# First norm from whole rows, roots by a square root and one Newton step, last product and store by tile, another order of recurrence pieces

## The chip, the cores and the metric

The kernel runs on one core of a Trainium2 chip. The metric is the device time of one execution in microseconds (us), taken as the median of several runs. Lower is better.

## The reference

A model of four blocks works on x of 512 tokens by 1024 values, all in float32. Each block is a mixer and then a feed-forward network, both behind a root-mean-square norm and both added to the running state h:

```python
for i in range(DEPTH):
    hn = rmsnorm(h, norm_mix[i])
    m = [rwkv7_mix, swa_sink_mix, sgu_chunk_mix, gla_mix][i](hn, ...)
    h = h + m
    h = h + swiglu(rmsnorm(h, norm_ffn[i]), ffn_w_in[i], ffn_w_out[i])
return rmsnorm(h, norm_final)

def rmsnorm(x, g):
    y = x * lax.rsqrt(jnp.mean(jnp.square(x), -1, keepdims=True) + 1e-5)
    return y * g
```

The first mixer holds a recurrence over the 512 tokens with 16 heads of 64; it is the part whose order of work is changed. The norm in front of it, and the norm behind the last feed-forward network, are the other two places of the change.

## The kernel before, in words

**Recorded and planned.** The program is first recorded: every operation becomes an object with its engine, its operands and an estimated cost. Then `Program.run` (lines 301 to 421) plans: it gives out the operations one by one, each time the one that can start earliest by its estimates, and on a tie the one recorded first. What it gives out is the order in which each engine then runs its own instructions, one after the other. So a line that is recorded earlier or later moves instructions on all engines. All recorded operations have line 239 in the profile. The planner also puts unneeded products of the identity matrix (line 525, called fillers below) on TensorE where it expects a gap, so that the engine's clock stays up.

**Split products.** Each float32 operand is split into a high part (a cast on ScalarE, tile `whi` or `slot`) and a low part (a subtraction on VectorE, tile `wlo` or `slot`), and `mm3` (line 613) makes three products of them. The feed-forward networks and three projections multiply 2 by 2 blocks with seven products in place of eight (`seven`, line 865). `x22` is the last of the seven; it is added into the PSUM tiles `p` of the two products before it, one for each of two token tiles b.

**First norm.** `token_squares` (line 755) loads x (token by feature) in eight pieces of 128 by 512. ScalarE squares and sums six of them, VectorE takes the statistics of the two of the last token tile. The mean squares `ms` of four token tiles go through `rsqrt` (line 733): a starting value from the bits and three Newton steps, ten small VectorE operations one behind the other. `rstd` (line 778) spreads the result `rcol` over the partitions with four transposes on TensorE; x transposed (`x_t`, tiles `h`) is multiplied by it, and the first real products follow. Between them `load_cols` (line 562) brings the gain vectors: two DMAs, two TensorE transposes, two VectorE copies to `vec`.

**Recurrence.** Four groups n of four heads go through generators: `ahead(n)` prepares the decays and keys (tiles `ew`, `et`, `qk`, `kb`), `solve(n)` makes products (tiles `pa`, `pr`), inverts triangular blocks (first eight ScalarE copies of 32 partitions, `et<-pa` or `et<-pr`, then a chain of small VectorE operations), `rwkv_chain` steps the state through four chunks (tiles `wu`, `vu`, `tok`, `st`), and `rwkv_out` norms its result (tiles `out`). The string `ORDERS[n]` (line 31) tells in which order these generators are advanced while group n's chain runs: c is a step of the chain, o a half of the output, p a piece of `solve(n + 1)`, q a piece of `ahead(n + 2)`, f one of `ahead(n + 1)`.

**Last norm and store.** `finish` (line 670) squares and sums each finished half row of h on ScalarE. `store` (line 1990) takes the token tiles in two halves: `rcol` of two tiles, then for each tile the left half times `rcol` and gain on VectorE, the right half times `rcol` on ScalarE, and a DMA of 128 by 1024 to `out`.

Of the kernel before, what the change touches and what calls it, by code (L numbers as in the profile page):

```python
# [17 lines left out]
P = 128  # L18
S = 512
D = 1024  # L20
# [3 lines left out]
NB = S // P  # L24
EPS = 1e-5
SLOTS = 45
PARTS = ((4, 5), (0, 1), (2, 3))
WIDTHS = (512, 512, 512, 512, 384, 384)
TABLES = {AF.Exp: "exp", AF.Ln: "ln", AF.Sigmoid: "sigmoid", AF.Tanh: "tanh", AF.Silu: "silu", AF.Gelu: "gelu", AF.Sin: "sin"}
# [477 lines left out]
class K:  # L507
# [84 lines left out]
        return self.ps.tile([P, S], F32, name="ps")  # L592


    def weights(self, view, nk, n, pool=False):
# [9 lines left out]
        (nc.gpsimd if pool else nc.vector).tensor_sub(lo[:, :m], raw[:, :m], hi[:, :m])  # L605
        r = lambda t: t[:, :m].rearrange("p (k n) -> p k n", k=nk)
        return r(hi), r(lo)

# [136 lines left out]
    def rcol(self, b0=0, b1=NB):  # L745

        nc = self.nc
        ms, col = [self.sm.tile([P, NB], F32, name=n)[:, :b1 - b0] for n in ("ms", "rcol")]
        ss = self.ss.rearrange("p (b n) -> p b n", b=NB)[:, b0:b1, :]
        nc.vector.tensor_add(ms, ss[:, :, 0], ss[:, :, 1])  # L750
        nc.vector.tensor_scalar(ms, ms, 1.0 / D, EPS, op0=ALU.mult, op1=ALU.add)
        self.rsqrt(col, ms)
        return col

    def token_squares(self):


        nc = self.nc
        ss, ms = self.sm.tile([P, 2 * NB], F32, name="ss2"), self.sm.tile([P, NB], F32, name="ms")
        st, mv = self.lay.tile([P, 2, 6], F32, name="xst"), self.lay.tile([P, 2], F32, name="xmv")  # L760
        for j in range(2):
            for b in range(NB):
                x = self.slot()
                nc.sync.dma_start(x, self.d['x'][b * P:(b + 1) * P, j * S:(j + 1) * S])
                if b == NB - 1:
                    nc.vector.bn_stats(st[:, j, :], x)
                else:
                    nc.scalar.activation(x, x, AF.Square, accum_out=ss[:, 2 * b + j:2 * b + j + 1])
        nc.vector.bn_aggr(mv, st)
        s2 = ss.rearrange("p (b n) -> p b n", b=NB)  # L770
        l = NB - 1
        nc.vector.scalar_tensor_tensor(ms[:, l:], mv[:, 0:1], mv[:, 0:1], mv[:, 1:2], op0=ALU.mult, op1=ALU.add)
        nc.vector.tensor_scalar(ms[:, l:], ms[:, l:], EPS, None, op0=ALU.add)
        nc.vector.tensor_add(ms[:, :l], s2[:, :l, 0], s2[:, :l, 1])
        nc.vector.tensor_scalar(ms[:, :l], ms[:, :l], 1.0 / D, EPS, op0=ALU.mult, op1=ALU.add)
        return ms

    def rstd(self, ms=None):


        nc = self.nc
        if ms is None:
            col = self.rcol()
        else:
            col = self.sm.tile([P, NB], F32, name="rcol")
            self.rsqrt(col, ms)
# [58 lines left out]
    def out_fast(self, w, nsub, x, last):  # L845

        nc = self.nc
        where = {'m1': [(0, 0, 1)], 'm2': [(0, 0, 1)], 'm5': [(1, 1, -1), (0, 1, -1)], 'm3': [(0, 1, -1)], 'm6': [(0, 1, -1)],
                 'm7': [(1, 1, -1)], 'm4': [(1, 0, 1)]}
        for name, ps in self.seven(w, S, x, nsub):  # L850
# [14 lines left out]
    def seven(self, w, W, x, nsub=4):  # L865

# [7 lines left out]
        nc = self.nc  # L874
        us = [(k, min(2, nsub - k)) for k in range(0, nsub, 2)]
# [11 lines left out]
                nc.gpsimd.dma_start(t, w[q][:, k * W:(k + n) * W], accum_op=ALU.add)  # L887

        def mm(key, ps, raw, first, last):
            xs = x(key)  # L890
# [22 lines left out]
        b = load(2)  # L913
        add(b, 0)
        r = banks()
# [101 lines left out]
    def rwkv(self, g, g_next, slots):  # L1017
# [16 lines left out]
        xq, tp = self.pool("xq", 8, tall), self.pool("tp", 3, tall)  # L1034

        hn = self.h
        ms = self.token_squares()
# [952 lines left out]
    def store(self):  # L1990

        nc = self.nc
        for half in range(2):
            col = self.rcol(half * 2, half * 2 + 2)
            for j in range(2):
                b = half * 2 + j
                l, r = self.h[b][:, :S], self.h[b][:, S:]
                nc.vector.scalar_tensor_tensor(l, l, col[:, j:j + 1], self.g[0], op0=ALU.mult, op1=ALU.mult)
                nc.scalar.activation(r, r, AF.Identity, scale=col[:, j:j + 1])
                nc.sync.dma_start(self.d['out'][b * P:(b + 1) * P, :], self.h[b])  # L2000


# [143 lines left out]
```

## Time and profile before

| what | value |
|---|---|
| time, median of 3 runs | 2394.17 us (2392.96 to 2395.63) |
| span of the profiled execution | 2393.6 us |
| instructions | 36634 |
| TensorE (PE) busy | 2352.7 us, 98% |
| VectorE (DVE) busy | 1934.0 us, 81% |
| ScalarE (ACT) busy | 1437.0 us, 60% |
| GpSimd (POOL) busy | 326.3 us, 14% |
| bytes moved by DMA | 404.23 MB, 169 GB/s on average |

The profiled execution has no separate timing: its own time is known by its span, 2393.6 us, which is 0.57 us below the median of the runs and lies among them.

How to read the rows that follow in the prediction. In the order of time (the timeline) a row is: start in us from the span's start, duration in us, engine, line, operation, what it writes, what it reads, how many; in brackets at the end the idle time of the engine before it and what ended that. A float32 product of the identity shows as two records. In the table by stages a row is: from and to, length, then for each engine its busy time and count, then the granted clock of TensorE (1.00 is full), the busy share of the DMA engines and GB/s. In the chain of waits a row is: start, duration, and the engine and tile on which the end of the program hung then. In the groups a row is: operation and shapes, count, busy us, mean ns of one.

### The profile page before, as it was taken

What the parts mean: (1) busy time and instruction counts of PE and PEld (TensorE: products, weight loads), DVE (VectorE), ACT (ScalarE), POOL (GpSimd) and SP (SyncE); (2) the same over time, 40 slices, a digit from 0 to 9 for tenths busy, and PEclk for the clock granted to TensorE, in tenths of its full rate; (3) what the DMA queues carried; (4) which work ended last, traced back from release to release, by engine and by line L of the source; (5) the groups of instructions that cost most, each with busy time, mean ns of one, the idle gap of its engine ahead of it and who ended that gap; (6) DMA issues with size and microseconds to landing.
All of it is one profiled execution on the core that took longest, in us unless ns stands there. A gap on an engine that the chain in (4) does not pass through costs nothing.

```text
span 2393.6 us, 36634 instructions
## 1 busy us (share of the span) xinstructions
PE 2352.7 (98%) x13524; PEld 1925.6 (80%) x13524; DVE 1934.0 (81%) x3261; ACT 1437.0 (60%) x2514; POOL 326.3 (14%) x398
## 2 busy tenths in 40 slices
PE   9999889999999999999999999999999999999998
PEld 8577777988888769888887888888888778988886
DVE  8577987887889878878699888886869978886868
ACT  4476765755556587555575444755557737755555
POOL 0000000221211001211111101121121101121110
PEclk9999999999999999999999999999999999999999
DMA  5220012998998326999988664899898758899985
GB/s 174 71 77 13 8 66 65 214 217 221 220 213 202 88 65 156 211 234 217 215 217 212 187 157 100 197 210 227 219 216 210 166 134 171 203 204 233 218 207 118
DMA packets 127603, 404.23 MB, mean 169 GB/s; under 512 B 14400, under 2 KB 17984, under 8 KB 127424
## 3 DMA queue, kind: packets, MB, share of 16 engines
q0 software_dynamic: 51840, 176.18, 41.2%
q1 hardware_dynamic: 75584, 225.72, 28.1%
q8 instruction: 106, 1.74, 0.3%
q14 instruction: 73, 0.60, 0.1%
HBM read 397.39 MB, written 2.10 MB: 167 GB/s over the span
## 4 chain that ended last, share of the span: by engine, by line
PE 83%; DVE 6%; ACT 5%; DMA 4%; issue 2%; SPq 0%; POOL 0%; DVEq 0%; ACTq 0%; POOLq 0%
PE ps L239 83%; DVE slot L239 2%; ACT slot L239 2%; DMA wraw<-ffn_w_a 2%; DMA wraw<-ffn_w_b 1%; DVE wlo L239 1%; ACT et L239 1%; ACT whi L239 1%; DVE h L239 1%; ACT vu L239 0%; ACT wu L239 0%; DMA wraw<-sg_w_o 0%; ACT L239 0%; DVE left L239 0%; DMA slot<-x 0%
## 5 line engine op out<-in xcount | busy, mean ns | idle before, releaser
L239 PE MATMUL ps<-whi,slot 128*128 128x512 f32 (+1 forms) x5072 | 1554.2, 384 | 3.6 <-DVE slot L239 3.1
L239 PEld LDWEIGHTS ps<-whi,slot 128*128 128x128 f32 x5072 | 943.3, 188 | 179.2 <-ACT whi L239 8.0
L239 ACT CAST whi<-wraw 128x1024 fp32r<-128x1024 f32 (+3 forms) x843 | 688.3, 836 | 565.4 <-PE ps L239 432.9
L239 DVE TENSOR_TENSOR wlo<-wraw,whi 128x1024 fp32r<-128x1024 f32 (+3 forms) x843 | 790.5, 954 | 256.6 <-ACT whi L239 254.8
L239 PE MATMUL ps<-wlo,slot 128*128 128x512 f32 (+1 forms) x2536 | 968.9, 382 | 1.8 <-DVE wlo L239 1.8
L239 PEld LDWEIGHTS ps<-wlo,slot 128*128 128x128 f32 x2536 | 476.5, 188 | 86.5 <-DVE wlo L239 6.6
L239 PE MATMUL ps<-slot,whi 128*128 128x512 f32 x688 | 217.1, 395 | 1.0 <-ACT slot L239 1.0
L239 DVE TENSOR_TENSOR slot<-ps,slot 128x512 f32<-128x512 f32 (+2 forms) x271 | 161.0, 608 | 48.4 <-PE ps L239 33.9
L239 ACT CAST slot<-left 128x512 fp32r<-128x512 f32 (+1 forms) x294 | 164.6, 589 | 53.4 <-PE ps L239 29.5
L239 DVE TENSOR_TENSOR slot<-left,slot 128x512 fp32r<-128x512 f32 (+1 forms) x294 | 183.4, 644 | 10.8 <-ACT slot L239 6.9
L239 DVE TENSOR_TENSOR h<-h,ps 128x512 f32<-128x512 f32 x240 | 159.7, 683 | 27.7 <-PE ps L239 25.2
L239 POOL DMA_DIRECT2D wraw<-ffn_w_a x128 | 109.7, 860 | 497.8 <-DVE wlo L239 415.1
L239 PEld LDWEIGHTS ps<-slot,whi 128*128 128x128 f32 x688 | 127.7, 188 | 32.7 <-DVE slot L239 2.6
L239 PE MATMUL ps<-slot,wlo 128*128 128x512 f32 x344 | 133.9, 391 | 0.0
L239 POOL DMA_DIRECT2D wraw<-ffn_w_b x64 | 54.9, 864 | 419.9 <-DVE slot L239 119.9
L239 ACT COPY slot<-ps 128x512 f32<-128x512 f32 (+1 forms) x144 | 78.4, 562 | 39.0 <-PE ps L239 36.9
L239 POOL DMA_DIRECT2D wraw<-ffn_o_a x64 | 54.6, 853 | 285.6 <-DVE wlo L239 151.9
L239 ACT COPY left<-ps 128x512 f32<-128x512 f32 x108 | 54.8, 558 | 57.0 <-PE ps L239 57.0
L239 PE MATMUL ps<-ident,slot 128*128 128x128 f32 x561 | 85.8, 277 | 0.9 <-DVE slot L239 0.6
L239 PEld LDWEIGHTS ps<-ident,slot 128*128 128x128 f32 x561 | 63.3, 140 | 26.0 <-DVE slot L239 12.9
L239 PEld LDWEIGHTS ps<-slot,wlo 128*128 128x128 f32 x344 | 64.5, 188 | 14.2 <-DVE wlo L239 0.8
L239 DVE SCALAR_TENSOR_TENSOR slot<-slot,ncol 128x512 f32<-128x512 f32 (+1 forms) x96 | 65.1, 701 | 9.2 <-ACT slot L239 9.0
(302 smaller groups left out, 2070.2 us busy)
## 6 DMA issues: line engine op xcount, KB each, us to landing
wraw<-ffn_w_a SPq DMA_DIRECT2D x128, 512.0 KB, 6.6
wraw<-ffn_w_a POOLq DMA_DIRECT2D x128, 512.0 KB, 6.9
wraw<-ffn_o_a SPq DMA_DIRECT2D x64, 512.0 KB, 5.1
wraw<-ffn_o_a POOLq DMA_DIRECT2D x64, 512.0 KB, 7.3
wraw<-ffn_w_b SPq DMA_DIRECT2D x64, 384.0 KB, 3.9
wraw<-ffn_w_b POOLq DMA_DIRECT2D x64, 384.0 KB, 6.4
wraw<-gla_w_p SPq DMA_DIRECT2D x24, 512.0 KB, 4.9
wraw<-gla_w_p POOLq DMA_DIRECT2D x24, 512.0 KB, 6.3
```

The lines of the kernel that those rows point to most:

```text
L239: op = self.add(eng.name, lambda: getattr(eng.target, what)(*map(real, args), **{k: real(a) for k, a in kw.items()}), *self.price(eng.name ...
```

## The change

Three places are changed.

**First norm.** x is loaded in four whole rows of 128 by 1024 into tiles of the pool `rk`. ScalarE squares tiles 0 and 2 whole; VectorE takes the statistics of tile 1; of tile 3 VectorE takes the left half and ScalarE the right. A new function `root` replaces `rsqrt` at this norm and at the last: ScalarE's square root, then on VectorE a reciprocal and one Newton step (four small operations). A one-element square root is put in front, so that the square root's table is loaded first.

**Last product and store.** In the very last feed-forward product the matmuls of `x22` are recorded with all of token tile 0 ahead of token tile 1. `store` takes the tiles as (0, 1), (2) and (3), each group with its own `root`.

**Order.** `ORDERS` changes for groups 0, 1 and 2.

```diff
-ORDERS = "ffppcpqcpqqcopcopcoo", "ppcpqcpqqcopcopcoo", "ppcpcpcopcopcoo", "cccococ"
+ORDERS = "ffppcpqcpqqcocppocoo", "ppcpqcqpqcopcpcooo", "ppcpccpopcopcoo", "cccococ"
...
+    def root(self, ms):
...
+        n = ms.shape[-1]
+        col, t = [self.sm.tile([P, NB], F32, name=x)[:, :n] for x in ("rcol", "root")]
+        nc.scalar.activation(t, ms, AF.Sqrt)
+        nc.vector.reciprocal(col, t)
+        nc.vector.tensor_mul(t, col, col)
+        nc.vector.scalar_tensor_tensor(t, ms, -0.5, t, op0=ALU.mult, op1=ALU.mult)
+        nc.vector.scalar_tensor_tensor(col, t, 1.5, col, op0=ALU.add, op1=ALU.mult)
+        return col
+
+    def token_squares(self, rows):
...
+        for b in range(NB):
+            x = rows[b]
+            nc.sync.dma_start(x, self.d['x'][b * P:(b + 1) * P, :])
+            if b % 2 == 0:
+                nc.scalar.activation(x, x, AF.Square, accum_out=ss[:, b:b + 1])
+            elif b == 1:
+                for j in range(2):
+                    nc.vector.bn_stats(st[:, j, :], x[:, j * S:(j + 1) * S])
+                nc.vector.bn_aggr(mv[:, 0, :], st)
+            else:
+                late = self.lay.tile([P, 1, 6], F32, name="xlate")
+                nc.vector.bn_stats(late[:, 0, :], x[:, :S])
+                nc.scalar.activation(x[:, S:], x[:, S:], AF.Square, accum_out=ss[:, b:b + 1])
+                nc.vector.bn_aggr(mv[:, 1, :], late)
...
-                for b in range(2):
-                    for k in range(n):
-                        c = slice(k * W, (k + 1) * W)
-                        self.mm3(ps[b], *self.pick(xs, k0 + k, b), hi[:, c], lo[:, c], first and k0 + k == 0, last and k0 + k == nsub - 1)
+                sides = [(b, k0 + k, hi[:, k * W:(k + 1) * W], lo[:, k * W:(k + 1) * W]) for b in range(2) for k in range(n)]
+                if end and key == 'x22':
+                    held += sides
+                    sides = sorted(held, key=lambda x: x[0]) if u == len(us) - 1 else []
+                for b, k, h, l in sides:
+                    self.mm3(ps[b], *self.pick(xs, k, b), h, l, first and k == 0, last and k == nsub - 1)
...
+        rows = [keepers.tile([P, 2 * S], F32, name="rk") for _ in range(NB)]
+        nc.scalar.activation(self.sm.tile([P, NB], F32, name="root")[:, :1], self.onec, AF.Sqrt)
+        ms = self.token_squares(rows)
...
-        for half in range(2):
-            col = self.rcol(half * 2, half * 2 + 2)
-            for j in range(2):
-                b = half * 2 + j
+        for b0, b1 in ((0, 2), (2, 3), (3, 4)):
+            col = self.root(self.mean_squares(b0, b1))
+            for b in range(b0, b1):
```

What the planner makes of it at the places of which the prediction speaks follows; a row is the line, the operation, what it writes and reads, the shape, and how often in a row.

VectorE at the program's start, before: the two copies of the gain vectors (`vec`) stand in the middle of the mean squares (`ms`), and ten small operations from `rcol` to `rcol` follow.

```order
L239 BN_AGGR xmv<-xst 128x2
L239 TENSOR_SCALAR ms<-ms 128x3
L239 SCALAR_TENSOR_TENSOR ms<-xmv 128x1
L239 COPY vec<-ps 128x128
L239 TENSOR_SCALAR ms<-ms 128x1
L239 COPY vec<-ps 128x128
L239 TENSOR_SCALAR rcol<-ms 128x4
L239 TENSOR_TENSOR rs_t<-rcol 128x4
```

The same place now:

```order
L239 BN_AGGR xst_147<-xlate 128x2
L239 COPY vec<-ps 128x128
L239 SCALAR_TENSOR_TENSOR ms<-xst_147 128x1
L239 COPY vec<-ps 128x128
L239 TENSOR_SCALAR ms<-ms 128x1
L239 SCALAR_TENSOR_TENSOR ms<-ss_132,ms 128x1
L239 RECIPROCAL rcol<-root 128x4
L239 TENSOR_TENSOR root<-rcol 128x4
L239 SCALAR_TENSOR_TENSOR root<-ms,root 128x4
L239 SCALAR_TENSOR_TENSOR rcol<-root,rcol 128x4
```

The copies of `vec` still stand in front of the last three steps to `ms`; behind them four operations are left in place of ten, and the reciprocal waits for ScalarE's square root. On TensorE the 33 fillers at the program's start still stand ahead of the two transposes that these copies read.

ScalarE in the recurrence, as the chain of group 1 begins (`et<-pa` are the copies for the inversion, `et<-ew` and `ew<-ew` belong to the preparation, `wu` and `vu` to the chain), before:

```order
L239 COPY vu<-ps 64x256
L239 ACTIVATE et<-pa,mk 32x16x16
L239 COPY et<-pa 32x16x16
L239 COPY out<-ps 128x256
L239 ACTIVATE et<-pa,mk 32x16x16
L239 COPY et<-pa 32x16x16
L239 ACTIVATE wu<-st_1206,pend 128x128
L239 ACTIVATE et<-pa,mk 32x16x16
L239 ACTIVATE wu<-st_1206,pend 128x128
L239 COPY vu<-ps 64x256
L239 ACTIVATE et<-ew 128x512 x2
L239 ACTIVATE ew<-ew,ka_1211,vec 128x512
```

The same place now:

```order
L239 ACTIVATE et<-ew 128x512 x2
L239 ACTIVATE ew<-ew,ka_1199,vec 128x512
L239 ACTIVATE out<-ps,vec 128x256 x2
L239 COPY et<-pa 32x16x16 x2
L239 ACTIVATE wu<-st_1188,pend 128x128 x2
L239 CAST rk<-out 128x256 x2
L239 COPY vu<-ps 64x256
L239 ACTIVATE et<-pa,mk 32x16x16 x2
L239 COPY out<-ps 128x256
L239 COPY et<-pa 32x16x16 x2
L239 ACTIVATE et<-pa,mk 32x16x16 x2
```

The three operations of the preparation moved from behind the copies `et<-pa` to ahead of them. Some 45 us earlier, in the chain of group 0, TensorE had these rows before:

```order
L239 MATMUL ps<-vu,tok 64x64 x4
L239 MATMUL ps<-wu,iv 64x64 x8
L239 MATMUL ps<-st_1175,qk 64x128 x4
L239 MATMUL ps<-v_1360,pr 64x64 x3
L239 MATMUL ps<-vu,tok 64x64 x4
```

and has these now:

```order
L239 MATMUL ps<-vu,tok 64x64 x4
L239 MATMUL ps<-wu,iv 64x64 x5
L239 MATMUL ps<-st_1163,qk 64x128
L525 MATMUL ps<-ident 128x128 x3
L239 MATMUL ps<-st_1163,qk 64x128 x3
L239 MATMUL ps<-wu,iv 64x64 x3
L239 MATMUL ps<-vu,tok 64x64 x4
```

Three fillers moved in between the chain's products with the state. Over the recurrence the planner places 30 fillers where it placed 28.

At the program's end ScalarE had, behind the last four squares, only the four scalings of `h`. Now it has:

```order
L239 ACTIVATE slot,ss_22907<-h 128x512 x4
L239 ACT_TABLE_LOAD
L239 ACTIVATE root<-ms 128x2
L239 ACTIVATE root<-ms 128x1
L239 ACTIVATE h<-h,rcol 128x512 x3
L239 ACTIVATE root<-ms 128x1
L239 ACTIVATE h<-h,rcol 128x512
```

The table load and all three square roots stand behind the square of the last tile. On TensorE the sorted `x22` comes out of the planner nearly as it was: of its 24 matmuls one stands two places further ahead (the first of the third weight piece into the first token tile), and the first token tile is still complete six matmuls ahead of the second, as before.

More of the change, by code (lines that the diff above doesn't have):

```diff
@@ L28 @@
 WIDTHS = (512, 512, 512, 512, 384, 384)
-TABLES = {AF.Exp: "exp", AF.Ln: "ln", AF.Sigmoid: "sigmoid", AF.Tanh: "tanh", AF.Silu: "silu", AF.Gelu: "gelu", AF.Sin: "sin"}
+TABLES = {AF.Exp: "exp", AF.Ln: "ln", AF.Sigmoid: "sigmoid", AF.Tanh: "tanh", AF.Silu: "silu", AF.Gelu: "gelu", AF.Sin: "sin", AF.Sqrt: "sqrt"}
 ALSO = {"exp": ("tanh",), "sigmoid": ("tanh",), "silu": ("sin", "tanh"), "gelu": ("tanh",)}
-ORDERS = "ffppcpqcpqqcopcopcoo", "ppcpqcpqqcopcopcoo", "ppcpcpcopcopcoo", "cccococ"
+ORDERS = "ffppcpqcpqqcocppocoo", "ppcpqcqpqcopcpcooo", "ppcpccpopcopcoo", "cccococ"
 LOCAL = "qqqqqaqaqaqaoaoooaoaoaoo"
@@ L592, in bank, with weights @@
         return self.ps.tile([P, S], F32, name="ps")
-    def weights(self, view, nk, n, pool=False):
+    def weights(self, view, nk, n):
         nc = self.nc
@@ L604, in weights @@
         nc.scalar.copy(hi[:, :m], raw[:, :m])
-        (nc.gpsimd if pool else nc.vector).tensor_sub(lo[:, :m], raw[:, :m], hi[:, :m])
+        nc.vector.tensor_sub(lo[:, :m], raw[:, :m], hi[:, :m])
         r = lambda t: t[:, :m].rearrange("p (k n) -> p k n", k=nk)
@@ L743, in rsqrt, with mean_squares @@
             nc.vector.scalar_tensor_tensor(y, t, 1.5, y, op0=ALU.add, op1=ALU.mult)
-    def rcol(self, b0=0, b1=NB):
+    def mean_squares(self, b0, b1):
         nc = self.nc
-        ms, col = [self.sm.tile([P, NB], F32, name=n)[:, :b1 - b0] for n in ("ms", "rcol")]
+        ms = self.sm.tile([P, NB], F32, name="ms")[:, :b1 - b0]
         ss = self.ss.rearrange("p (b n) -> p b n", b=NB)[:, b0:b1, :]
@@ L751, in rcol @@
         nc.vector.tensor_scalar(ms, ms, 1.0 / D, EPS, op0=ALU.mult, op1=ALU.add)
+        return ms
+    def rcol(self):
+        ms, col = self.mean_squares(0, NB), self.sm.tile([P, NB], F32, name="rcol")
         self.rsqrt(col, ms)
         return col
-    def token_squares(self):
+    def root(self, ms):
         nc = self.nc
-        ss, ms = self.sm.tile([P, 2 * NB], F32, name="ss2"), self.sm.tile([P, NB], F32, name="ms")
-        st, mv = self.lay.tile([P, 2, 6], F32, name="xst"), self.lay.tile([P, 2], F32, name="xmv")
-        for j in range(2):
[L762 to L775, printed above, removed]
@@ new lines, in root @@
+        n = ms.shape[-1]
[7 more added lines that the diff above has]
+    def token_squares(self, rows):
+        nc = self.nc
+        ss, ms = self.sm.tile([P, NB + 1], F32, name="ss1"), self.sm.tile([P, NB], F32, name="ms")
+        st, mv = [self.lay.tile([P, 2, n], F32, name=f"xst{n}") for n in (6, 2)]
+        for b in range(NB):
[12 more added lines that the diff above has]
+                nc.vector.bn_aggr(mv[:, 1, :], late)
+        nc.vector.scalar_tensor_tensor(ms[:, 1:2], mv[:, 0, 0:1], mv[:, 0, 0:1], mv[:, 0, 1:2], op0=ALU.mult, op1=ALU.add)
+        nc.vector.tensor_scalar(ms[:, 1:2], ms[:, 1:2], EPS, None, op0=ALU.add)
+        nc.vector.tensor_scalar(ms[:, 0:3:2], ss[:, 0:3:2], 1.0 / D, EPS, op0=ALU.mult, op1=ALU.add)
+        m = ms[:, 3:4]
+        nc.vector.scalar_tensor_tensor(m, mv[:, 1, 0:1], mv[:, 1, 0:1], mv[:, 1, 1:2], op0=ALU.mult, op1=ALU.add)
+        nc.vector.tensor_scalar(m, m, 0.5, EPS, op0=ALU.mult, op1=ALU.add)
+        nc.vector.scalar_tensor_tensor(m, ss[:, 3:4], 1.0 / D, m, op0=ALU.mult, op1=ALU.add)
@@ L784, in rstd @@
         else:
-            col = self.sm.tile([P, NB], F32, name="rcol")
-            self.rsqrt(col, ms)
+            col = self.root(ms)
         ps = self.bank()
@@ L849, in out_fast @@
                  'm7': [(1, 1, -1)], 'm4': [(1, 0, 1)]}
-        for name, ps in self.seven(w, S, x, nsub):
+        for name, ps in self.seven(w, S, x, nsub, last and self.kind == 'final'):
             for half, nh, sign in where[name]:
@@ L863, in pick, with seven @@
         return [t_[:, t] for t_ in xs[k // 2]]
-    def seven(self, w, W, x, nsub=4):
+    def seven(self, w, W, x, nsub=4, end=False):
         nc = self.nc
@@ L889, in mm @@
         def mm(key, ps, raw, first, last):
-            xs = x(key)
+            xs, held = x(key), []
             for u, (k0, n) in enumerate(us):
@@ L1036, in rwkv @@
         hn = self.h
-        ms = self.token_squares()
+        rows = [keepers.tile([P, 2 * S], F32, name="rk") for _ in range(NB)]
+        nc.scalar.activation(self.sm.tile([P, NB], F32, name="root")[:, :1], self.onec, AF.Sqrt)
+        ms = self.token_squares(rows)
         v = self.v = self.load_cols()
@@ L1992, in store @@
         nc = self.nc
-        for half in range(2):
-            col = self.rcol(half * 2, half * 2 + 2)
-            for j in range(2):
-                b = half * 2 + j
+        for b0, b1 in ((0, 2), (2, 3), (3, 4)):
+            col = self.root(self.mean_squares(b0, b1))
+            for b in range(b0, b1):
                 l, r = self.h[b][:, :S], self.h[b][:, S:]
-                nc.vector.scalar_tensor_tensor(l, l, col[:, j:j + 1], self.g[0], op0=ALU.mult, op1=ALU.mult)
-                nc.scalar.activation(r, r, AF.Identity, scale=col[:, j:j + 1])
+                nc.vector.scalar_tensor_tensor(l, l, col[:, b - b0:b - b0 + 1], self.g[0], op0=ALU.mult, op1=ALU.mult)
+                nc.scalar.activation(r, r, AF.Identity, scale=col[:, b - b0:b - b0 + 1])
                 nc.sync.dma_start(self.d['out'][b * P:(b + 1) * P, :], self.h[b])
```

## Prediction

> **What bounds the kernel now.** I read the page first, then the table by stages, then the timeline at the start, the recurrence and the end, then the chain of waits in the recurrence. The page, and the stages that matter:
>
> ```profile
> PE 2352.7 (98%) x13524; PEld 1925.6 (80%) x13524; DVE 1934.0 (81%) x3261; ACT 1437.0 (60%) x2514; POOL 326.3 (14%) x398
> ```
>
> ```profile
> 230.00:270.00 40.00, 38.80 (x627) 30.32 (x625) 36.43 (x109) 29.53 (x67) 2.58 (x4) 0.91 0.04 12
> 270.00:300.00 30.00, 24.41 (x366) 18.87 (x367) 27.27 (x77) 22.71 (x52) 0.00 (x0) 1.00 0.01 1
> 353.00:430.00 77.00, 75.95 (x746) 59.91 (x743) 61.96 (x135) 43.49 (x103) 1.88 (x2) 1.00 0.29 85
> 600.00:2340.00 1740.00, 1732.18 (x8326) 1428.58 (x8325) 1414.27 (x2210) 1047.74 (x1790) 272.96 (x322) 1.00 0.80 190
> ```
>
> TensorE is busy 98% of the span, and 1732.18 of 1740 us between 600 and 2340. There no other engine can gain anything, and the change doesn't touch it: a gain or loss ahead of it shifts it whole. What is touched is the start (TensorE waits for the first norm), the recurrence, where TensorE is idle 5.59 us of 30 between 270 and 300, and the end, where the last norm and the store follow TensorE's last product. From 353 on TensorE is full again, so a piece of the recurrence counts only as far as it shortens TensorE's waits before that. About 0.2% of the time, 4.8 us, is what a measurement of this kernel can tell from no change. The span is 2393.6 us, 0.57 below the median of 2394.17; I sum against the span and add the 0.57.
>
> **The start.** The timeline there:
>
> ```profile
> 9.37 1.28 PE L525 MATMUL ps<-ident 128*128 128x128 f32 x10
> 10.17 0.69 DVE L239 BATCH_NORM_STATS2 xst<-slot 128x6 f32<-128x512 f32 x1 [2.56 <-DMA slot<-x]
> 10.48 0.46 PE L239 MATMUL ps<-ident,vraw 128*128 128x128 f32 x2
> 11.28 0.28 DVE L239 COPY vec<-ps 128x128 f32<-128x128 f32 x1
> 11.74 0.16 DVE L239 TENSOR_SCALAR rcol<-ms 128x4 int32<-128x4 int32 x1
> 11.93 0.16 DVE L239 TENSOR_TENSOR rs_t<-rcol 128x4 f32<-128x4 f32 x1
> 13.50 0.16 DVE L239 SCALAR_TENSOR_TENSOR rcol<-rs_t,rcol 128x4 f32<-128x4 f32 x1
> ```
>
> The last piece of x lands at 10.17 and the ten operations end at 13.50 + 0.16. Whole rows are the same bytes in half as many DMAs; they can land earlier, but that is worth little: VectorE's order puts both copies of `vec` ahead of the last steps to `ms`, and these copies wait for transposes that stand on TensorE behind 33 fillers, which run without a gap up to 10.48. So the chain now starts at the first transpose's end, 10.48 + 0.28, about 10.8, however early x is there. From there: copy, step, copy, step, step at 0.2 each (11.74 to 11.93 is the pace of a dependent pair, 0.06 when independent) end at about 11.65; the square root on ScalarE; reciprocal and three steps. The two new operations have close relatives in the groups, and the table load is there too:
>
> ```profile
> L239 ACT ACT_TABLE_LOAD x22 | 28.2, 1283 | 1.1 <-PEq L2138 0.8
> L239 ACT ACTIVATE se<-se 128x8 f32<-128x8 f32 x8 | 1.7, 215 | 3.0 <-DVE se L239 3.0
> L239 DVE RECIPROCAL smx<-smx 128x8 f32<-128x8 f32 x8 | 1.6, 201 | 0.2
> ```
>
> So root 0.22 plus two hand-overs of 0.04, then 4 x 0.2 = 0.8: `rcol` is there at about 12.75, against 13.66. **Start: -0.9.** Bounds: if x still lands at 10.17, the statistics, the two copies and the three steps behind them (0.69 + 0.2 + 1.0) start the root at 12.05, 0.4 later, so -0.5; if the independent steps all pass at 0.06, -1.2. TensorE's first products and what follows them move by the same amount, since each waits for VectorE. The price of the square root's table is one more table load ahead of the later tanh:
>
> ```profile
> 87.52 0.59 ACT L239 ACTIVATE twa<-ps 64x512 f32<-64x512 f32 x1
> 91.04 1.05 ACT L239 CAST whi<-wraw 128x1024 fp32r<-128x1024 f32 x1 [2.93 <-PE ps L239]
> ```
>
> It stands right ahead of the row at 87.52, and ScalarE idles 2.93 us behind it waiting for TensorE: a load of 1.28 us is covered. **Table load: 0**; without the cover it would be 1.28.
>
> **The end.** Timeline, then the DMA side:
>
> ```profile
> 2381.24 0.69 DVE L239 TENSOR_TENSOR h<-h,ps 128x512 f32<-128x512 f32 x1 [0.45 <-PE ps L239]
> 2382.63 0.69 DVE L239 TENSOR_TENSOR h<-h,ps 128x512 f32<-128x512 f32 x1 [0.44 <-PE ps L239]
> 2383.35 0.63 ACT L239 ACTIVATE slot<-h 128x512 f32<-128x512 f32 x1 [0.66 <-DVE h L239]
> 2383.88 0.19 ACT L239 ACTIVATION_READ_ACCUMULATOR slot<-h 128x1 f32 x1
> 2384.60 1.41 DVE L239 SCALAR_TENSOR_TENSOR h<-h,rcol,slot 128x512 f32<-128x512 f32 x2
> 2385.41 4.08 SPq L239 DMA_DIRECT2D out<-h  x4
> 2387.68 1.41 DVE L239 SCALAR_TENSOR_TENSOR h<-h,rcol,slot 128x512 f32<-128x512 f32 x2
> ```
>
> ```profile
> 2391.00:2392.00 1.00, 0.00 (x0) 0.00 (x0) 0.00 (x0) 0.00 (x0) 0.00 (x0) 0.50 0.93 365
> 2392.00:2393.60 1.60, 0.00 (x0) 0.00 (x0) 0.00 (x0) 0.00 (x0) 0.00 (x0) 0.50 0.00 0
> ```
>
> The sorted last product changes nothing: the order shows one matmul moved by two places, so the first token tile is still ready at 2381.24 and the second at 2382.63. Before, the first two tiles were scaled at 2384.60, from a chain that ran on VectorE while TensorE finished. Now all roots wait on ScalarE behind the last square: 2383.88 + 0.19 = 2384.07, plus a table load of 1.28 is 2385.35, plus the root 0.22 and the hand-over is 2385.6. Two interleaved chains of four end at about 2386.5; three scalings at 0.68 occupy VectorE to about 2388.5; then the last tile's chain: two steps 0.4, root 0.26, four steps 0.8, so its scaling starts at about 2390.0. The last of the four scalings before started at 2387.68 + 0.66 = 2388.34: 1.6 later. Of this the DMAs give some back. Before, two tiles were in flight together and the transfers ended near 2391.9, 1.7 us before the span's end (the two stages above). A tile's DMA is issued 0.8 us behind its scaling's start (2384.60 to 2385.41) and moves 512 KB in 1.3 us at full share (365 GB/s at a share of 0.93). Now three tiles flow from about 2388, which ends near 2391.9, and the last tile follows alone at once: 2393.2. **End: +1.3.** Bounds: +0.9 if the last tile, issued at 2390.8, starts 0.7 us after that, +1.6 if nothing is given back.
>
> A rule of the Trainium skill speaks against this change. The page "ScalarE: Activation LUTs", section "What ACT_TABLE_LOAD costs", gives a table load as about 1283 ns and a drain of about 1380 ns on top of it at every switch; the end would be 1.38 longer by it, an estimate from that page. The row of 22 loads agrees with the first number. The rows around one of them show no drain, since the next operation starts at 213.68 + 1.29:
>
> ```profile
> 213.06 0.62 ACT L239 COPY et<-kkrs 128x512 f32<-128x512 f32 x1
> 213.68 1.28 ACT L239 ACT_TABLE_LOAD   x1
> 214.97 1.26 ACT L239 ACTIVATE ew<-ps,vec 128x512 f32<-128x512 f32 x2
> ```
>
> **The recurrence.** Here the planner decides, and what can be costed are two places. The first is the saturated run of ScalarE, in the chain of waits (the rows between are ScalarE's too):
>
> ```profile
> 275.76 0.71 ACT rk L239 x2
> ...
> 284.83 1.16 ACT et L239 x2
> 286.01 0.81 ACT ew L239
> ...
> 288.15 0.48 PE ps L239 x8
> ```
>
> From 275.76 to 288.15 the path is ScalarE alone. The three operations at 284.83 and 286.01, 1.16 + 0.81 = 1.97 us, now stand ahead of the run, where ScalarE waits for others:
>
> ```profile
> 272.33 1.02 ACT L239 ACTIVATE out<-ps,vec 128x256 f32<-128x256 f32 x2 [1.97 <-PE ps L239]
> 274.83 0.37 ACT L239 COPY wu<-ps 128x256 f32<-128x256 f32 x1 [1.48 <-PE ps L239]
> ```
>
> Idle 1.97 and 1.48 us hide them: -2.0. The second place is the three fillers in group 0's chain:
>
> ```profile
> 227.60 0.49 PE L525 MATMUL ps<-ident 128*128 128x128 f32 x2 [2.68 <-ACT tok L239]
> 230.40 1.12 PE L239 MATMUL ps<-st,qk 128*64 128x128 f32 x8
> 232.31 0.69 PE L239 MATMUL ps<-vu,tok 128*64 128x64 f32 x8 [0.17 <-ACT vu L239]
> ```
>
> ```profile
> 230.00:232.00 2.00, 1.97 (x24) 1.40 (x20) 1.51 (x7) 1.98 (x6) 0.00 (x0) 0.51 0.00 0
> 234.00:236.00 2.00, 2.00 (x32) 1.55 (x30) 1.93 (x9) 1.55 (x5) 0.00 (x0) 0.50 0.00 0
> ```
>
> After a wait of 2.68 us TensorE ran at half its clock from 230 to 237. A filler (two records) took 0.49 there, so three take 1.5, and only 0.17 us of idle time covers them: +1.3, unless the chain waits there for ScalarE anyway. Sum: **recurrence -0.7**. This is the weakest term. On the gain side the ceiling is all of TensorE's idle time from 270 to 300, 5.6 us; on the other side stands the half clock, rival two.
>
> **Sum.** -0.9 + 0 + 1.3 - 0.7 = -0.3 against the span, 2393.3; plus 0.57 the forecast is 2393.9, no change that can be told.
>
> **The rivals.**
>
> *Faster: the new order fills the gaps.* Chain steps now come ahead of outputs, and with ScalarE's run broken up TensorE's 5.6 us of idle time between 270 and 300 may go altogether. For it speaks that VectorE, the next engine there (27.27 of 30 busy), has 2.7 us of its own to give; against it, that this caps the gain near 2.7 unless VectorE's work moves out of the stretch too. With -5.6 in place of -0.7: 2389.0.
>
> *Slower: a second stretch at half clock.* One wait of 2.68 us with little behind it was enough for 7 us at half clock. TensorE's waits for the copies of the next inversion, at 276 to 289, are of that kind; if the new order puts two of them together, TensorE's 81% load there becomes more than the half clock can carry. Each us at half clock then costs 0.81, less the idle time swallowed (about 1.5): from 8 us on, 8 x 0.81 - 1.5 = +5.0, it is slower by over 0.2%; at 14 us (two such stretches) +8.7 less 0.9 of wait, so about 2401.7. Against it: the planner puts eleven fillers at the start of that chain, where it had five. The Trainium skill's page "TensorE: Matmul & The Clock Gate", section "Part 1: The HAM clock gate", says that the gate falls after an idle window of about 3.4 us and that this window runs free; the wait here was shorter, so this trace goes further than the rule.
>
> *The drain is paid at the end.* 1.38 more, 2395.3, by the rule above; the rows show none.
>
> *The order does nothing on balance.* Then -0.9 + 1.3 remain: 2394.6.
>
> **How the numbers follow.** Forecast 0.55, faster rival 0.20, slower rival 0.10, drain 0.10, no effect of the order 0.05. The time is the first one's, 2393.9. The range reaches down nearly to the faster rival (its last part left out) and up by the start's -0.5, the end's +1.6, and a short stretch at half clock of 3.5 us beyond the forecast: 2389.6 to 2398.1. Faster by over 0.2% (under 2389.4) takes the faster rival and 0.02 of the forecast's tail, slower (over 2399.0) the slower rival and 0.01: 0.22, 0.67, 0.11.
>
> **What would show it.** Right: in the changed profile the `rcol` transposes at about 12.8; TensorE's last product as far ahead of the span's end as sums to 12.3 where it was 11.0 (2382.6 to 2393.6); the last scaling 1.6 later behind it; ScalarE's run in group 1 shorter by 2 us. Wrong: a granted clock of 0.5 in another stage, TensorE idle under 2 us from 270 to 300, or transposes of `rcol` before 12, which would mean that the fillers didn't hold the copies.

## The result, and the profile after

The changed kernel takes 2399.77 us in the median of 15 runs (2395.3 to 2404.07), the kernel before beside it 2394.72 us (15 runs, 2392.96 to 2396.47). The ratio is 1.0021, with a 95% interval from 1.0014 to 1.0028: slower by 5.05 us, where no change that can be told was forecast. The 15 runs fall apart by TensorE's mean granted clock: three with 0.997 took 2395.3 to 2395.8 us, twelve with 0.994 or 0.995 took 2398.1 to 2404.1. The kernel before has 0.997 in nearly all of its runs.

The profiled execution is the longest of the 15 (2404.07 us, span 2402.3, 8.7 more than before). Of these 8.7, 1.9 us lie between two of ScalarE's table loads at 1264.0 and 1538.2, far behind the places of the change: 274.1 us for 272.2, and 272.0 to 273.3 in all other profiles. Another 1.7 us lie between the second of these loads and TensorE's last product (852.1 us for 850.5). Both look like that execution's own and not the change's; without them it is near the median. The page's line for the engines, then the stage between 270 and 300:

```profile
PE 2359.8 (98%) x13522; PEld 1930.1 (80%) x13522; DVE 1937.1 (81%) x3253; ACT 1439.7 (60%) x2515; POOL 328.0 (14%) x398
```

```profile
270.00:300.00 30.00, 26.42 (x329) 21.51 (x325) 24.35 (x74) 18.62 (x42) 0.00 (x0) 0.83 0.01 1
```

Between 270 and 300 TensorE is busier than before (26.42 us, was 24.41) and yet further behind: its clock there is 0.83, was 1.00. VectorE and ScalarE do less in the same time (24.35 and 18.62 us, were 27.27 and 22.71): they wait. The same table at a grain of 1 us shows the two places:

```profile
275.00:276.00 1.00, 0.48 (x10) 0.37 (x6) 1.00 (x3) 0.00 (x0) 0.00 (x0) 0.91 0.00 0
...
279.00:280.00 1.00, 1.00 (x20) 0.84 (x18) 0.00 (x0) 0.94 (x3) 0.00 (x0) 0.88 0.00 0
...
289.00:290.00 1.00, 0.81 (x15) 0.57 (x12) 0.98 (x3) 0.97 (x4) 0.00 (x0) 0.74 0.00 0
...
296.00:297.00 1.00, 1.00 (x6) 0.82 (x5) 0.75 (x2) 0.95 (x4) 0.00 (x0) 0.85 0.00 0
```

A clock of 0.91 in one microsecond is 0.18 us at half clock, so the first stretch runs from 275.82 to 279.24 (3.42 us) and the second, by 0.74 and 0.85, from 289.48 to 296.30 (6.82 us). The chain of waits shows what both did, and the three fillers of group 0 ahead of them:

```profile
231.14 1.58 PE ps L525 x6
...
275.72 2.38 PE ps L525 x10
...
282.01 0.71 ACT rk L239 x2
...
289.08 0.38 ACT wu L239
...
289.50 12.72 PE ps L239 x171
```

ScalarE's run, 275.76 to 288.15 before, now lasts from 282.01 to 289.46: it did get shorter. But it begins 6.3 us later, behind VectorE's steps and then five fillers that stand in the path for 2.38 us, in the first stretch at half clock. And behind it the path is 12.72 us of TensorE, half of it at half clock, where before it was one short row of products.

The start, in order of time:

```profile
1.43 9.87 PE L525 MATMUL ps<-ident 128*128 128x128 f32 x66 [1.43 <-POOL ident L239]
8.64 0.69 DVE L239 BATCH_NORM_STATS2 xlate<-rk 128x6 f32<-128x512 f32 x1
11.14 0.38 PE L239 MATMUL ps<-ident,vraw 128*128 128x128 f32 x2
11.45 0.29 DVE L239 COPY vec<-ps 128x128 f32<-128x128 f32 x1 [1.90 <-PE ps L239]
13.29 0.16 DVE L239 SCALAR_TENSOR_TENSOR rcol<-root,rcol 128x4 f32<-128x4 f32 x1
13.51 0.65 PE L239 MATMUL ps<-ident,rcol 128*128 128x128 f32 x4 [0.20 <-DVE rcol L239]
```

x has landed by 8.64, VectorE waits 1.90 us for the transposes behind the fillers, and `rcol` is there at 13.45: 0.2 us earlier than before, not 0.9. The 33 fillers ended 0.66 us later than before (11.14 against 10.48), because TensorE left its slow first microseconds later. The number of matmul records in one microsecond tells it, first before, then after:

```profile
5.00:6.00 1.00, 1.00 (x11) 1.00 (x10) 0.00 (x0) 1.00 (x4) 0.00 (x0) 1.00 0.80 272
```

```profile
5.00:6.00 1.00, 1.00 (x7) 1.00 (x6) 0.00 (x0) 0.51 (x2) 0.00 (x0) 1.00 0.99 385
6.00:7.00 1.00, 1.00 (x10) 1.00 (x9) 0.91 (x2) 0.00 (x0) 0.00 (x0) 1.00 1.04 414
```

TensorE keeps 10 or 11 records a microsecond from then on; before it had reached that pace at 5 us, after only at 6. (The clock's column shows 1.00 in all three rows, so it doesn't tell this.)

The end, in order of time:

```profile
2389.89 0.40 PE L239 MATMUL ps<-whi,slot 128*128 128x512 f32 x1
2391.77 1.28 ACT L239 ACT_TABLE_LOAD   x1
2393.07 0.30 ACT L239 ACTIVATE root<-ms 128x2 f32<-128x2 f32 x2
2394.09 2.08 DVE L239 SCALAR_TENSOR_TENSOR h<-h,rcol,slot 128x512 f32<-128x512 f32 x3
2394.90 3.72 SPq L239 DMA_DIRECT2D out<-h  x4
2397.48 0.75 DVE L239 SCALAR_TENSOR_TENSOR h<-h,rcol,slot 128x512 f32<-128x512 f32 x1
```

From the last product's end (2390.29) to the span's end are 12.0 us, before 11.0. Root and load stand where the forecast had them, and the last scaling starts 7.19 us behind the last product (before 5.74, so 1.45 later; forecast 1.6).

For the recurrence two of ScalarE's table loads serve as marks, one ahead of it and one behind. Before, then after:

```profile
122.66 1.28 ACT L239 ACT_TABLE_LOAD   x1
...
447.23 1.28 ACT L239 ACT_TABLE_LOAD   x1
```

```profile
122.47 1.28 ACT L239 ACT_TABLE_LOAD   x1
...
451.62 1.28 ACT L239 ACT_TABLE_LOAD   x1
```

324.6 us became 329.2: the recurrence lost 4.6 us where a gain of 0.7 was forecast. This interval, "between the marks" below, is a sharp measure: five profiles that lay out the recurrence as before, with the same fillers there, have 324.1 to 324.6.

### The profile page after: what moved, and what is told of

It is laid out like the page before. It is cut to its first block, busy times and chain, and to the rows that moved or that the text cites. A ratio compares the mean times of both kernels' runs of the same rounds, so it can differ in the third digit from the quotient of the medians.

```text
span 2402.3 us, 36627 instructions
## 1 busy us (share of the span) xinstructions
PE 2359.8 (98%) x13522; PEld 1930.1 (80%) x13522; DVE 1937.1 (81%) x3253; ACT 1439.7 (60%) x2515; POOL 328.0 (14%) x398
## 4 chain that ended last, share of the span: by engine, by line
PE 85%; DVE 6%; ACT 5%; DMA 2%; issue 1%; POOL 0%; ACTq 0%; POOLq 0%; DVEq 0%
PE ps L239 84%; DVE slot L239 2%; DMA wraw<-ffn_w_b 2%; ACT slot L239 2%; DVE wlo L239 1%; ACT et L239 1%; PE ps L525 1%; ACT whi L239 1%; DVE h L239 0%; DMA wraw<-ffn_w_a 0%; DVE left L239 0%; ACT wu L239 0%; DVE mt L239 0%; ACT L239 0%; ACT vu L239 0%
```

## The experiments

**Which part of the change.** The listings show something that the prediction had not asked: with only the new start, and the old strings, the planner also lays out the recurrence anew, since it works with absolute times and the start is shorter by its estimates. So there are three new layouts: by the strings, by the start, and by both (the changed kernel). The first kernel has only the strings:

```diff
-ORDERS = "ffppcpqcpqqcopcopcoo", "ppcpqcpqqcopcopcoo", "ppcpcpcopcopcoo", "cccococ"
+ORDERS = "ffppcpqcpqqcocppocoo", "ppcpqcqpqcopcpcooo", "ppcpccpopcopcoo", "cccococ"
```

> The kernel before with only the three new strings of ORDERS; start and end are as before. Theory 'clock': the new order of recurrence pieces leaves stretches of some 3.4 us in which TensorE has little to do, the granted clock halves behind them, and that is the whole loss; then the median is 2397 to 2401 us, the mean clock of most runs 0.994 or 0.995 where before has 0.997, and the runs are spread over some 8 us. Rival 'start': the planner lays the recurrence out anew because the start is shorter, and the strings matter little; then the median is within 1 us of 2394.7.

Measured: 2402.43 us (5 runs, 2401.39 to 2408.36; before 2395.20), ratio 1.0038 (1.0024 to 1.0052), 330.3 us between the marks. By the median the strings alone lose more than the whole change, though the intervals of the two ratios overlap. The clock was 0.993 to 0.996; beside the 6.8 us that the kernel before has too, the profile has two stretches of 3.4 us at half clock, at 286 and 337.

The second has only the new norm (`token_squares`, `root`, `rows` as in the change).

> The kernel before with only the new first norm (whole rows, square root, one Newton step); strings, last product and store as before. The listing of its instructions shows that the planner lays out the recurrence differently although the strings are the old ones. Theory 'clock, by the strings': 2394.5 +- 0.7 us (the changed profile has rcol 0.2 us earlier), clock 0.997. Rival 'start': the new layout by itself has the empty stretches; 2397 us or more, clock 0.995 or less in most runs.

Measured: 2403.89 us (5 runs, 2402.22 to 2406.43; before 2395.20), ratio 1.0038 (1.0026 to 1.0051). The rival holds: an edit of the first 14 us makes the kernel 8.7 us slower, between 200 and 450 us. Its marks, 333.3 us apart:

```profile
121.86 1.28 ACT L239 ACT_TABLE_LOAD   x1
...
455.17 1.28 ACT L239 ACT_TABLE_LOAD   x1
```

**Is it the planning?** The same norm, and the planner told that it takes as long as the old one:

```diff
             col = self.root(ms)
+            nc.ops[-1].lat += 1245.0
```

> The kernel before with the new first norm, and with one number more: the planner is told that the last step of this norm takes 1.245 us longer than it does, so that it plans everything behind it as in the kernel before. TensorE's rows are then the old ones from the first to the last; beside the start, VectorE, ScalarE and SyncE keep their old order too. The instructions of the norm are those of the run with only the start. Theory 're-planning': the loss of the start alone, 8.7 us, is all in the other layout of the recurrence, so 2394.0 to 2395.2 us, clock 0.997. Rival 'the norm itself' (its transfers, its table load ahead of twa): 2398 us or more.

Measured: 2394.12 us (11 runs, 2391.75 to 2397.85; before 2394.59), ratio 0.9999 (0.999 to 1.0008). One number in the planner's estimate, which changes no operation of the program but only their order and the fillers, takes the 8.7 us away:

```profile
122.17 1.28 ACT L239 ACT_TABLE_LOAD   x1
...
446.28 1.28 ACT L239 ACT_TABLE_LOAD   x1
```

In this profile the clock rose at 5.0 us, about as before, and the last step of `rcol` ended at 12.90, 0.76 earlier than before. The transposes of `rcol` stand behind eleven fillers there and come at 13.27, 0.45 earlier than before.

**Is it the clock?** First with more fillers where the changed kernel's TensorE waits, 19 and then 10, put in when the order is already made, so that nothing else moves:

```diff
-    NEAR = 80
+    NEAR, more = 80, lambda self, i, t: i in {2113: 2, 2121: 4, 2135: 2, 2141: 2, 2147: 2, 2245: 7} and min(self.warm[0].slots["ps"].free, default=1e9) < t and self.warm[1]({2113: 2, 2121: 4, 2135: 2, 2141: 2, 2147: 2, 2245: 7}[i])
...
-            cost = op.cost
+            self.more(order, s); cost = op.cost
```

A pair is an operation's place in the plan and the fillers ahead of it: 2113 to 2135 are products on `rk`, 2245 the product with `wu` that waits at 286.5 us.

> The changed kernel with 19 more fillers on TensorE at six places where it waits between 268 and 288 us; nothing else moves on any engine. Theory 'clock': no granted clock of 0.5 between 268 and 300, the median falls to 2394 to 2397 us, the runs lie within 3 us of each other. Rival 'chain': the new order makes the chain of dependent steps itself longer; then the time stays at 2399 to 2401 us, or rises by up to 4 us, since 19 fillers at 0.22 us stand in the chain.

Measured: 2398.89 us (11 runs, 2396.62 to 2401.86), clock 0.996 or 0.997, no half clock between 268 and 300, 328.3 us between the marks. The clock was mended and the time hardly: neither theory's numbers, though the time is just below the rival's.

The same with the table `{2113: 1, 2121: 3, 2135: 1, 2245: 5}`:

> The changed kernel with 10 fillers more between 268 and 288 us, half of those of the run with 19, so that they fit TensorE's waits there better; nothing else moves. In the changed kernel's 15 runs the three with a clock of 0.997 took 2395.3 to 2395.8 us, the twelve with 0.994 and 0.995 took 2398.1 to 2404.1. Theory 'clock': the clock is 0.996 or 0.997 in nearly all runs and the median falls to 2395.5 to 2397.5 us. Rival 'chain': the clock rises and the time stays within 1 us of 2399.8.

Measured: 2401.61 us (11 runs, 2396.51 to 2404.25). The clock fell to 0.993 to 0.995 in nine runs; in the profile it was at half for 13.7 us from 272.6 on. The expectation failed: ten fillers didn't hold the clock. The median is 1.8 us above the changed kernel's, which is within the spread of the two.

Why fillers are no test was seen with the same tool on the kernel before, with the table `{1608: 10, 1613: 2, 1624: 1}`, ten of 13 at its wait of 2.68 us:

> The kernel before with 13 fillers more on TensorE between 225 and 230 us, ten of them in its wait of 2.68 us for ScalarE; nothing else moves. The clock of 0.5 for 6.83 us behind that wait stands in every profile so far. Theory 'the half clock costs': by the kernel without nine fillers (17 us more at half clock, 2.9 us later at the same place of the program) its price is 0.17 us per us, 1.2 us here; by the runs of the changed kernel, 1.3 to 1.5 us per stretch of 3.41 us, it is 2.5 to 3 us. So 2391.5 to 2393.5 us at a clock of 0.998 or 0.999. Rival 'TensorE isn't what the chain waits for here': the clock rises and the time stays at 2394.6 +- 0.5 us.

Measured: 2398.32 us (11 runs, 2397.35 to 2401.47), ratio 1.0019 (1.0009 to 1.0028): 3.6 us slower, with half as much half clock in the profile. The timeline there:

```profile
227.59 4.57 PE L525 MATMUL ps<-ident 128*128 128x128 f32 x22 [2.67 <-ACT tok L239]
...
232.09 0.43 PE L239 MATMUL ps<-ew,sel 128*32 128x128 f32 x8
```

The fillers wait 2.67 us themselves, for ScalarE's copy of `tok`: they need a PSUM bank, and it comes free with that copy. So they stand behind the wait that they were to fill, 4.57 us in the chain; the product that stood at 228.15 comes at 232.09. The filler at 227.60 in the prediction's rows had shown this: it too waited for `tok`.

The other way round, the kernel before without nine of its fillers (those at four places between 276 and 287 us):

```diff
-            call(n)
+            self.fills in (73, 76, 78, 81) or call(n)
```

> The kernel before without nine of its fillers, at four places between 276 and 287 us; nothing else moves. Theory 'clock': TensorE's stretches there become as empty as in the changed kernel, the clock halves in most runs, the median is 2396 to 2400 us and the clock 0.994 to 0.996. Rival 'chain': work that nothing needs is taken out of the chain, 2393.5 to 2395 us.

Measured: 2396.54 us (11 runs, 2393.8 to 2399.03), ratio 1.0006 (0.9997 to 1.0015). The profile has 17 us more at half clock and 327.4 us between the marks, 2.8 more. Within its runs, clocks of 0.997 go with 2393.8, 2394.2 and 2396.5 us, 0.994 with 2396.9, 2398.0 and 2399.0. So half clock seems to cost, about 0.17 us per us here, far less than the 0.81 of the prediction's rival. The ratio's interval includes 1, and the nine fillers' own time went with them, so the price may be higher.

The clean test brings in TensorE work that needs no bank. In the changed kernel two products issue again into the bank that they have just written (each starts the bank anew, so the values are the same), and a group of fillers that waits for nothing grows by six:

```diff
-            op.call()
+            for _ in range({2113: 6, 2127: 3}.get(order, 1)): op.call()
...
-            call(n)
+            call(n + {80: 6}.get(self.fills, 0))
```

> The changed kernel with more TensorE work between 268 and 288 us that needs no further PSUM bank: two of the products on rk issued 6 and 3 times in place of once (the same values into the same place), and six fillers more in the group of six ahead of the wait for wu. About 0.7 us of that stands ahead of TensorE's wait at 271 us, 1.3 us ahead of its wait of 1.6 us at 286.5. Theory 'half clock': the clock is 0.996 or 0.997 in most runs, and these take 2395 to 2397.5 us. Rival 'chain': the clock rises in most runs and the median stays at 2399.8 +- 1 us. If the clock doesn't rise (0.994, 0.995), the run tells nothing.

Measured: 2397.54 us (11 runs, 2395.52 to 2398.5), ratio to before 1.001 (1.0001 to 1.0018), clock 0.996 or 0.997 in every run. Stage and marks of this profile:

```profile
270.00:300.00 30.00, 28.39 (x406) 23.62 (x406) 27.75 (x83) 20.54 (x47) 0.00 (x0) 1.00 0.01 2
```

```profile
123.04 1.28 ACT L239 ACT_TABLE_LOAD   x1
...
449.19 1.28 ACT L239 ACT_TABLE_LOAD   x1
```

The half clock between 270 and 300 is gone, and with it 2.2 us of the median and all runs above 2398.5; between the marks 3.0 us of the 4.6 (326.2). So those two stretches are about two thirds of what the recurrence lost, and 1.6 us are left. The upper end of the expectation is just missed.

Where they are left is told by VectorE's first update of the state `st` in group 1 and in group 2. Before, then the changed kernel, then this run:

```profile
277.46 0.58 DVE L239 COPY st<-ps 64x128 f32<-64x128 f32 x2
...
325.28 0.28 DVE L239 COPY st<-ps 64x128 f32<-64x128 f32 x1
```

```profile
278.57 0.27 DVE L239 COPY st<-ps 64x128 f32<-64x128 f32 x1
...
329.13 0.58 DVE L239 COPY st<-ps 64x128 f32<-64x128 f32 x2
```

```profile
279.47 0.27 DVE L239 COPY st<-ps 64x128 f32<-64x128 f32 x1
...
326.37 0.58 DVE L239 COPY st<-ps 64x128 f32<-64x128 f32 x2
```

| us | before | changed | this run |
|---|---|---|---|
| first mark to group 1 | 154.8 | 156.1 | 156.4 |
| group 1 to group 2 | 47.8 | 50.6 | 46.9 |
| group 2 to second mark | 122.0 | 122.5 | 122.8 |

The middle row holds the end of the first stretch and the whole second one: it was 2.7 us longer than before and is 0.9 shorter once they are gone, so taking them away brought 3.7 us there. What is left lies ahead, 1.6 us up to group 1, and 0.9 behind. This run's profile has a stretch of 3.4 us at half clock at 335 us, which the changed kernel's doesn't have, and loses only 0.3 more there.

The same in the kernel before, whose four transposes of `qk` ahead of the wait at 225 us are issued four times:

> The kernel before with the four transposes of qk ahead of TensorE's wait of 2.68 us at 225 us issued four times each (12 more, some 1.6 us, the same values into the same bank). Theory 'half clock': the 6.83 us at half clock that follow in every profile of before become 3.41 or 0, and the time falls by 1 to 2.5 us, to 2392 to 2393.7 us. Rival 'TensorE isn't what the chain waits for': less half clock, and 2394.6 +- 0.5 us.

Measured: 2395.01 us (11 runs, 2391.89 to 2397.35), ratio 0.9998 (0.9989 to 1.0007). Five runs had 0.998, with a median of 2395.0, and five 0.997, with 2395.2. The profile still has the 6.8 us, so this run doesn't decide between the two: the half clock was not taken away in it.

**The term of +1.3.** The changed kernel without the three fillers in group 0's chain:

```diff
-            call(n)
+            self.fills == 63 or call(n)
```

> The changed kernel without the three fillers between the products with the state in group 0's chain, the term of +1.3 us in the prediction; nothing else moves. If the term is right: 2398.5 us (2398.0 to 2399.0). Rival 'the chain waits there for ScalarE anyway, or the clock falls for longer without them': 2399.4 us or more.

Measured: 2400.7 us (8 runs, 2398.41 to 2406.39), clock 0.992 to 0.995. No gain is seen; its spread of 8 us hides one of 1 us (the profile has 1.0 less between the marks). Group 1 begins 156.2 us behind the first mark, as late as with the fillers (156.1), but at 226 the profile has 10.2 us at half clock in place of 6.8, as the rival had it. So whether the fillers cost their 1.58 us in the path is not shown.

**The end.** Last product and store alone:

> The kernel before with only the new last product and store; everything ahead of the end keeps its place. By the changed profile TensorE's last product ends 12.0 us ahead of the span's end where it was 11.0: 2395.2 to 2396.2 us. Rival 'nothing': 2394.4 to 2395.0 us.

Measured: 2395.71 us (11 runs, 2393.39 to 2398.12; before 2394.59), ratio 1.0004 (0.9995 to 1.0013), so +1.1 where the forecast had +1.3, though the interval includes no change; in the profile 12.3 us from the last product to the end. Then with the square root's table loaded early:

```diff
         if self.kind == 'final':
+            if half == 0 and nh == 0:
+                nc.scalar.activation(self.sm.tile([P, NB], F32, name="root")[:, :1], self.ss[:, 0:1], AF.Sqrt)
```

> As the run with only the end, and a one-element square root on ScalarE behind the first square of the last norm, so that the square root's table is loaded some 25 us ahead of the end; the planner then puts the root of the first two tiles ahead of the last two squares. If the load and the root's place behind the last square are what the end waits for: last product to span's end 7.5 to 9 us, so 2391.2 to 2393.0 us. Rival 'the transfers bound the end' (5.4 us without a pause in the changed profile, whatever is in front): no better than the end of the kernel before, 2394.4 us or more.

Measured: 2392.89 us (11 runs, 2391.69 to 2395.68), ratio 0.9993 (0.9984 to 1.0002), 2.8 less than without the early load. Its end:

```profile
2378.96 0.20 ACT L239 ACTIVATE root<-ms 128x2 f32<-128x2 f32 x1 [2.56 <-DVE ms L239]
...
2380.51 0.39 PE L239 MATMUL ps<-whi,slot 128*128 128x512 f32 x1
...
2381.92 1.41 DVE L239 SCALAR_TENSOR_TENSOR h<-h,rcol,slot 128x512 f32<-128x512 f32 x2
2383.01 3.69 SPq L239 DMA_DIRECT2D out<-h  x4
...
2385.55 0.75 DVE L239 SCALAR_TENSOR_TENSOR h<-h,rcol,slot 128x512 f32<-128x512 f32 x1
```

The root of the first two tiles is done ahead of the last product, after 2.56 us in which ScalarE had idled, and the last scaling starts 4.65 us behind that product, where the changed kernel needs 7.19. From the product to the end are 9.9 us, more than the 7.5 to 9 expected: the last scaling and its transfer still take 5.3 us of them, as before.

**A version that beats both.** The pinned start, the new end with the early table, and 22 fillers at the program's start in place of 33 (`call(n if self.fills else 22)`), with the old strings:

> New start and new end with the recurrence planned as before (the planner told of 1.245 us more), the square root's table loaded early for the end, and 22 fillers in place of 33 at the program's start, so that the transposes of the gain vectors no longer stand behind fillers. Sum from the runs: 2394.6 - 1.7 (early table) - 0.5 (start) - 1.0 to 1.7 (fillers at the start: x has landed by 8.6 us, and rcol can be there at 11.3 to 12.0 in place of 12.9) = 2390.7 to 2391.4 us; 2390 to 2392. Rival: something else (the weights of the first product, a lower clock after fewer fillers) ends last at the start, 2392.0 to 2393.0.

Measured: 2390.98 us (11 runs, 2388.19 to 2395.71; before 2394.74), ratio 0.9986 (0.9977 to 0.9995). The sum from the runs held. Its start:

```profile
1.44 7.85 PE L525 MATMUL ps<-ident 128*128 128x128 f32 x44 [1.44 <-POOL ident L239]
...
9.12 0.38 PE L239 MATMUL ps<-ident,vraw 128*128 128x128 f32 x2
...
11.80 0.60 PE L239 MATMUL ps<-ident,rcol 128*128 128x128 f32 x4
```

`rcol` goes to TensorE at 11.80, 1.9 us ahead of before, though the clock rose late here, at 7 us. The same with the 13 fillers at 225 us:

> The same with the 13 fillers at 225 us. If the half clock costs there what the theory says: 1.2 to 3 us less than without them. If not: the same within 0.5 us.

Measured: 2392.44 us (11 runs, 2390.63 to 2394.49), with a clock of 0.997 to 0.999. Neither of its two expectations holds: the median is 1.5 us higher, which is within the spread of the two, and the profile has 4.0 us more between the marks (328.2 for 324.2).

## Why the prediction was wrong, step by step

**Start, -0.9.** The mechanism held: x lands early and the fillers set the chain's start. The size depends on when in its first microseconds TensorE gets its full clock: -0.76 in a profile where that was as in the kernel before (start_pinned), -0.2 in the changed kernel's, where it came some 1.3 us later. The transposes were expected at about 12.8 and stand at 13.51; in two other profiles with the new start, only_start and after_less3, whose fillers end as early as before's (10.51 and 10.49), they stand at 12.88 and 12.85. The forecast's error is that it took the fillers' end as fixed: it lies between 10.48 and 11.83 in the profiles with 33 fillers. Where it is late, the new start gains only 0.4 us: 2.37 us from the first transposes to those of `rcol` (11.77 to 14.14 in after_rep), 2.76 with the old one (11.83 to 14.59 in before_rep).

**Table load, 0.** Held: the next mark, 35 us behind it, is 0.2 us earlier than before (122.47 against 122.66), as `rcol` is.

**End, +1.3.** Held: 12.0 us for 11.0 in the changed kernel, +1.1 us alone. ScalarE reads out the last square's sum until 2391.77, where the load begins; the load's end, 2393.05, and the root at 2393.07 leave no room for a drain either. The Trainium skill's page "ScalarE: Activation LUTs", section "What ACT_TABLE_LOAD costs", gives a drain of about 1380 ns on top of the load at each switch; these rows show none.

**Recurrence, -0.7.** This step failed: 4.6 us were lost, and in three ways the forecast didn't see it. First, it took the recurrence's new order to come from the strings and priced the start apart, while each of the two makes the planner lay out everything behind it anew: +8.7 us by the start, +7.2 by the strings, +5.0 by all together, and no change that can be told (-0.5) for the start once the planner's estimate is held. Second, it priced two places of a layout in which TensorE's rows had moved at many others. The -2.0 was real on ScalarE (its run ends 7.5 us after it begins, where it took 12.4), but the run began 6.3 us later and TensorE ended last behind it: from group 1 to group 2 it took 2.7 us more. With the new half clock taken away it takes 0.9 less than before, so part of the gain was there, under the loss. The +1.3 fits the 1.3 us lost up to group 1 and the 1.58 us of fillers in the path, but the run without the fillers doesn't confirm it; and its price of 0.49 was read at 227.60, where the clock was still full, so its size is luck. Third, the right mechanism stood among the rivals with a chance of 0.10: further stretches at half clock, one of them right behind the copies of the inversion, at 289. By the mean clock they came in twelve of 15 runs. The rows of TensorE could have warned of it, though no run shows that they are the reason: the 32 products on `rk`, which before had other products in between, stand in one row, with waits for VectorE in it.

The rival's price was too high as well. It gave 10.24 us at half clock 0.81 x 10.24 - 1.5 = 6.8 us; taking them away brought 3.7 from group 1 to group 2, 3.0 between the marks and 2.2 in the median. Two of the prediction's sums don't come out by its own price: 14 us at half clock are 14 x 0.81 - 1.5 = 9.8, not 8.7, and the upper end of its range counts 3.5 us at half clock as 3.5 in place of 2.8.

**What stays open.** Where the 1.3 to 1.6 us up to group 1 come from: the run after_rep has no more half clock there than the kernel before (6.8 us). How this fits the changed kernel's three runs at a clock of 0.997: they took 0.6 to 1.1 us more than the median of before, and start and end alone make 0.8 (-0.2 and +1.0), so that the recurrence seems to have lost next to nothing in them; none of them was profiled. And why the layouts by the start alone and by the strings alone lose 8.7 and 5.7 us between the marks, when their profiles have only 10.2 and 6.8 us more at half clock.

## What to carry to other kernels

Where a planner with absolute times sets the order, an edit anywhere changes the order everywhere behind it: compare the listings of each part of a change alone before pricing any, and hold the planner's estimate still when an edit is to be measured for itself. A filler that needs a buffer isn't free work for an idle engine: look at what it waits for. A table load that stands ahead of a short chain at the end belongs where its engine last idles.

## What the hardware showed beside that

The clock is decided in stretches of 3.41 us that don't begin with the program. In the changed kernel it fell at 228.04, 275.82 and 289.48, which are 47.78 and 13.66 us apart, 14 and 4 times 3.41. The rise at the start, by the number of TensorE's records in a quarter of a microsecond, came at 4.8 us in the profile of before and at 7.6 in that of before_rep, which begins with the same instructions. This agrees with the Trainium skill's page "TensorE: Matmul & The Clock Gate", section "Part 1: The HAM clock gate" (a window of 3413 ns that runs free). What it says of the fall, after an idle window, doesn't fit: TensorE was busy in every one of these windows. Three of the changed kernel, then two of the kernel before:

```profile
272.41:275.82 3.41, 2.66 (x29) 2.27 (x28) 3.41 (x11) 0.00 (x0) 0.00 (x0) 1.00 0.00 0
269.00:272.41 3.41, 2.60 (x32) 2.43 (x29) 3.41 (x10) 2.03 (x4) 0.00 (x0) 1.00 0.00 0
286.07:289.48 3.41, 1.65 (x28) 1.15 (x26) 2.80 (x6) 3.34 (x9) 0.00 (x0) 1.00 0.00 0
```

```profile
226.63:230.04 3.41, 1.81 (x32) 1.22 (x34) 2.68 (x6) 3.30 (x9) 0.00 (x0) 1.00 0.00 0
223.22:226.63 3.41, 1.71 (x37) 1.40 (x36) 3.38 (x7) 3.35 (x6) 0.00 (x0) 1.00 0.02 5
```

Behind the first the clock fell with TensorE busy 78% of the window, behind the second it stayed at 76%; before, it fell behind 53% and stayed behind 50%. So busy time alone, as the records have it, does not tell which window is too empty.
